# Two post-norm layers with a mixture of experts: norms and the last expert input on VectorE, the gates' parts behind the first gather, four more places for experts' weights

## The chip, the cores and the metric

The kernel runs as one program on one core of one Trainium2 chip. The metric is the device time of one execution in microseconds (us), the median of several runs. The engines are named as in the profile: PE (TensorE), PEld (its weight loads), DVE (VectorE), ACT (ScalarE), POOL (GpSimd) and SP (SyncE, which here only issues transfers).

## The reference

Two layers over 256 latent and 256 context tokens of width 1024. What follows the attention is what matters here:

```python
x = layer_norm(ALPHA * x + (1 + gate1) * o, ln1_g, ln1_b)       # ALPHA = 4 ** 0.25
u = x * (1 + scale2) + shift2                                   # input of the experts
if not last:                                                    # layer 0: context tokens too
    h_ctx = layer_norm(ALPHA * h_ctx + (1 + cgate1) * o_c, ln1_g, ln1_b)
    u_c = h_ctx * (1 + cscale2) + cshift2
f = moe_ffn(u, ...)        # 16 experts in 4 groups; best group, top 2 in it, gates normalised
x = layer_norm(ALPHA * x + (1 + gate2) * f, ln2_g, ln2_b)
```

In the experts, `hid = silu(xb @ w1[e]) * (xb @ w3[e])` and `y = (hid @ w2[e]) * gate`, in float32 with widths 1024, 512, 1024. Layer 0 sends 512 tokens through the experts, layer 1 only the 256 latent ones.

## The kernel before

A framework schedules the instructions by a model of their times; each engine and each transfer queue then works through its list in order, and waits at semaphores.

**Output projection and norm (`pre_moe`).** Tiles of 128 tokens, `n_out` of them (4 in layer 0, 2 in layer 1). For tile `t`, PE multiplies with `w_out` in two halves of 512 columns; its eight row blocks lie as split pairs: `wh`/`wl` (pool `wsp`, three pairs, blocks 0 to 2), `hl` in `ringb` (3 to 6) and `hl7` in pool `wos` (7). DVE builds the residual `z`. `post_norm` takes mean and variance of `z` (`stats`; ACT takes the square root), and writes three things: `u2` (the experts' input, with modulation; SP writes it to `u2d` in HBM, one transfer per tile), `xs` (the normed token, by ACT), and `xs` times ALPHA with the norm's gain and shift, which goes to `ysum` in HBM, where the experts' results are added. `lg` and `lb` hold the norm's gain and shift, multiplied by ALPHA on ACT beforehand. For all tiles but the last, the multiplication and addition of `xs` are done by POOL; for the last tile POOL makes `u2`, and DVE does `xs` later, after the first expert's indices (`keep["late"]` is ordered behind `keep["found"]`). `router` transposes `z` on PE, copies it on ACT (`zt`), and multiplies it with the router's weights into `lgt`; DVE turns that into `aff`.

**Routing (`route`).** A chain of small DVE instructions (`sel`, `hi`, `lo`, maxima, one-hots) gives the position of each token in its expert (`posm`) and the gates. The gates are cut into three bfloat16 parts by POOL (`auxg<-gate`), since PE sums them with one-hot matrices. For the first expert PE sums the tokens' numbers (`spare`), DVE turns them into indices (`ii`), and POOL gathers those rows of `u2d` with an indirect transfer (`xg<-u2d,ii`, the first gather). A one-element memset `mark` on POOL behind that gather releases transfers that are to come after it. Then all engines pass a branch (an overflow loop that isn't taken here).

**Experts (`moe`).** Weights come in units of 1024 KB, six per expert (two of each w1, w3, w2), 96 in a layer, loaded by SP (line 1303; 1289 for a unit in two halves) into places that take turns: 3 in `ring`, 4 in `ringu`, 4 in `ringb` (`n_slots` = 11), besides one unit in two halves in a `y` buffer and one in `xs`. The first 11 are issued before the gather: 10 as soon as their place is free, one (`PACE`) behind the last write of `u2d`. The unit in halves waits for `mark`, and all later units wait until a second `mark`, behind the second expert's gather, and the row of gates (`bcm`, or `xs<-modd` in layer 0) have been passed; each of these also waits until the unit four before it has landed (`DEPTH`). PE then multiplies: `ha`, `hb` (lines 1182, 1188) with w1 and w3, `ya`, `yb` with w2. PE's list has, ahead of the transposes of the first gather (`tp<-cst,xg`), the sums of the gates' parts (`ix<-auxg,oh`).

Of the kernel before, what the change touches and what calls it, by code (L numbers as in the profile page):

```python
# [17 lines left out]
F32 = mybir.dt.float32  # L18
# [5 lines left out]
ALU = mybir.AluOpType  # L24
# [4 lines left out]
P = 128  # L29
D = 1024  # L30
# [17 lines left out]
RING_B = 4  # L48
VECS_AHEAD = 2
# [3 lines left out]
PACE = (10, 11)  # L53
# [55 lines left out]
def layers(ctx: ExitStack, tc: tile.TileContext, x_in, x_ctx, c_in, w_in, w_out, w_ada, rows_in, lnv, sink, gains, rpbp,  # L109
# [344 lines left out]
    def pre_moe(l, sb, sr):  # L454
# [5 lines left out]
        with ExitStack() as st, ExitStack() as su:  # L460
# [429 lines left out]

            for tl in (lg, lb):
                S.mul(tl, tl, ALPHA)
# [35 lines left out]
            def post_norm(t, z):  # L928
# [3 lines left out]
                u2 = tmp.tile([P, D], F32, tag="u2", name="u2")  # L932
                if t < n_out - 1:
                    V.scalar_tensor_tensor(out=u2[:, half[0]], in0=z[:, half[0]], scalar=mean, in1=gg[:, half[0]],
                                           op0=ALU.subtract, op1=ALU.mult)
# [8 lines left out]
                else:  # L944

# [4 lines left out]
                    order(G.tensor_tensor(out=u2, in0=xs[:, t], in1=gg, op=ALU.mult), keep["normed"],  # L950
                          mybir.DependencyClass.NoSync)
                    G.tensor_tensor(out=u2, in0=u2, in1=bb, op=ALU.add)
                keep["u2 written"] = nc.sync.dma_start(u2d[t * P:(t + 1) * P], u2)
                eng = G if t < n_out - 1 else V
                keep["late"] = eng.tensor_tensor(out=xs[:, t], in0=xs[:, t], in1=lg, op=ALU.mult)
                keep["normed"] = eng.tensor_tensor(out=xs[:, t], in0=xs[:, t], in1=lb, op=ALU.add)
# [3 lines left out]
            def router(t, z, mean, y):  # L960
                r = t // 2
                for hf in range(2):
# [5 lines left out]
                    S.copy(zt, tp)  # L968
# [48 lines left out]
    def route(l, aff, nt, mp, ps):  # L1017
# [68 lines left out]
        V.tensor_tensor(out=gate, in0=chosen, in1=gsum.unsqueeze(2).to_broadcast(sh), op=ALU.mult)  # L1086
        for k in range(3):
            for r in range(nr):
                c = slice(2 * r, 2 * r + 2)
                part = aux[:, c, :, 2 + 3 * r + k]  # L1090
                G.tensor_copy(part, gate[:, c])
                if k < 2:
                    G.tensor_tensor(out=gate[:, c], in0=gate[:, c], in1=part, op=ALU.subtract)
# [160 lines left out]
    def moe(l, ringb, gen, rt, u2d, aff, nt, sb, ahead):  # L1254
        cap = CAP[l]
        with ExitStack() as st:
            mp = st.enter_context(tc.tile_pool(name="moe", bufs=1, side="right"))
            m1 = st.enter_context(tc.tile_pool(name="moe1", bufs=2))
# [18 lines left out]
            n_slots = RING_A + RING_U + RING_B  # L1277
# [6 lines left out]
            def eunit():  # L1284
                i = len(recent)
                src = order_of_use[loading[i]]
                if i == n_slots and Y_UNIT:
                    t = [gen.tile([P, D], F32, tag="y", name="w") for _ in range(2)]
                    d = [nc.sync.dma_start(t[k], src[:, k * 1024:k * 1024 + 1024]) for k in range(2)]
                    order(d[1], d[0], mybir.DependencyClass.NoSync)  # L1290
                    first_half.append(d[0])
                    d = d[1]
# [4 lines left out]

# [326 lines left out]
```

## Time and profile before

| | us |
|---|---|
| median of 3 runs (1178.72 to 1188.1) | 1181.44 |
| the profiled execution | 1177.92 |
| its span | 1176.1 |
| PE / DVE / ACT / POOL busy | 1047.7 / 524.5 / 333.5 / 291.4 |
| mean granted PE clock | 0.952 |

Layer 0 routes at 330 to 356 us and works through its experts until 637 us; layer 1 routes at 879 to 903 us, and its experts last until 1151 us. All times below are from the start of the span. In rows of a timeline the columns are start, duration, engine, line, operation, output and inputs, shape, count, and in brackets the idle time before and what ended it.

### The profile page before, as it was taken

How to read it: one execution, taken by the hardware profiler on the slowest of the kernel's cores; microseconds unless marked ns; L12 is line 12 of the kernel's file. 1: busy time of each engine (PE TensorE's matmuls, PEld its weight loads, DVE VectorE, ACT ScalarE, POOL GpSimd, SP SyncE). 2: the span in 40 equal slices, each digit the busy share in tenths (PEclk: the TensorE clock that was granted, in tenths of full speed). 3: DMA queues.
4: the chain of work that ended last, by engine and by line, in shares of the span. 5: the costliest groups of instructions: out<-in, count | busy, mean ns of one | idle time of the engine just before them, and what ended most of it. 6: DMA issues, size and time to landing. Idle time of an engine off the chain costs nothing. (4 is left out here: it accounts for less than half of the span.)

```text
span 1176.1 us, 21038 instructions
## 1 busy us (share of the span) xinstructions
PE 1047.7 (89%) x8651; PEld 606.3 (52%) x8652; DVE 524.5 (45%) x1207; ACT 333.5 (28%) x692; POOL 291.4 (25%) x250
## 2 busy tenths in 40 slices
PE   6999999999958999999996799999886998778875
PEld 4677666668844444444442578666663332223322
DVE  2435545655972444343333644655765221111114
ACT  1325457455221011011011543546531110000002
POOL 2000000100452434324313301001014453442242
PEclk9999999999968999999998799999985999998997
DMA  9854343856767999999996335656373999999992
GB/s 314 314 200 155 110 149 100 304 178 230 255 254 261 378 378 365 374 357 350 352 383 230 128 145 193 221 174 233 142 306 134 371 394 400 403 395 395 400 403 86
DMA packets 62161, 320.93 MB, mean 273 GB/s; under 512 B 14318, under 2 KB 18510, under 8 KB 28520
## 3 DMA queue, kind: packets, MB, share of 16 engines
q1 hardware_dynamic: 45120, 289.21, 64.6%
q0 software_dynamic: 11136, 23.30, 7.5%
q10 hardware_dynamic: 5800, 6.97, 1.8%
q8 instruction: 71, 1.16, 0.4%
q14 instruction: 34, 0.28, 0.1%
HBM read 310.40 MB, written 18.15 MB: 279 GB/s over the span
## 5 line engine op out<-in xcount | busy, mean ns | idle before, releaser
L1182 PE MATMUL ha<-w,xT 128*32 128x512 f32 (+1 forms) x1512 | 260.6, 615 | 31.1 <-DMA w<-in_w_dram 30.6
L1182 PEld LDWEIGHTS ha<-w,xT 128*32 128x32 f32 (+1 forms) x1512 | 77.0, 123 | 180.3 <-issue 120.7
L1209 ACT ACTIVATE hs<-ha 64x512 f32<-64x512 f32 x32 | 18.9, 591 | 417.5 <-PE ha L1182 417.5
L1182 PE MATMUL ya<-w,gT 128*32 128x512 f32 (+1 forms) x768 | 129.0, 597 | 4.0 <-DVE y L1229 1.6
L220 PE MATMUL pj<-wh,u 128*128 128x512 f32 (+2 forms) x256 | 95.5, 386 | 3.5 <-ACT wh L210 2.2
L221 PE MATMUL pj<-wl,u 128*128 128x512 f32 (+2 forms) x256 | 97.1, 380 | 0.7 <-DVE wl L211 0.7
L222 PE MATMUL pj<-wh,u 128*128 128x512 f32 (+2 forms) x256 | 94.1, 380 | 0.0
L1154 POOL MEMSET xg<- 96x1024 f32 (+1 forms) x32 | 30.2, 946 | 236.2 <-PE tp L1167 148.6
L1251 POOL DMA_INDIRECT ysum<-y,ii x30 | 44.4, 1479 | 154.8 <-DVE y L1232 105.7
L1229 DVE TENSOR_TENSOR y<-ya,gt 64x512 f32<-64x512 f32 x60 | 41.3, 688 | 84.9 <-PE ya L1182 77.3
L534 DVE TENSOR_REDUCE mx<-s 128x1 f32<-128x512 f32 (+1 forms) x80 | 54.8, 689 | 43.4 <-PE s L522 42.6
L1210 DVE TENSOR_TENSOR hs<-hs,ha 64x512 f32<-64x512 f32 x32 | 22.1, 690 | 114.3 <-ACT hs L1209 114.1
L545 ACT ACTIVATE p<-s,nm 128x512 f32<-128x512 f32 (+1 forms) x96 | 59.3, 623 | 37.4 <-DVE nm L541 21.5
L211 DVE TENSOR_TENSOR wl<-w,wh 128x1024 fp32r<-128x1024 f32 x38 | 46.0, 1222 | 48.7 <-ACT wh L210 48.7
L1182 PEld LDWEIGHTS ya<-w,gT 128*32 128x32 f32 (+1 forms) x768 | 35.1, 119 | 56.0 <-issue 46.9
L1188 PE MATMUL hb<-w,xT 128*32 128x256 f32 x1008 | 63.9, 379 | 0.0
L220 PEld LDWEIGHTS pj<-wh,u 128*128 128x128 f32 x256 | 48.6, 192 | 18.5 <-issue 4.3
L210 ACT CAST wh<-w 128x1024 fp32r<-128x1024 f32 x38 | 39.1, 1049 | 63.4 <-DMA w<-in_w_in_dram 40.3
L567 PE MATMUL o<-vt,pt 128*64 128x64 f32 x1280 | 52.5, 227 | 3.0 <-ACT pt L489 2.9
L221 PEld LDWEIGHTS pj<-wl,u 128*128 128x128 f32 x256 | 49.8, 194 | 10.4 <-DVE wl L211 1.9
L222 PEld LDWEIGHTS pj<-wh,u 128*128 128x128 f32 x256 | 49.3, 193 | 10.1 <-issue 1.1
L1237 POOL TENSOR_SCALAR gt<-xs,gs 96x1024 f32<-96x1024 f32 x16 | 53.5, 3341 | 0.0
(299 smaller groups left out, 1734.3 us busy)
## 6 DMA issues: line engine op xcount, KB each, us to landing
w<-in_w_dram SPq DMA_DIRECT2D x188, 1024.0 KB
w<-in_w_ada_dram SPq DMA_DIRECT2D x44, 1024.0 KB
w<-in_w_in_dram SPq DMA_DIRECT2D x16, 1024.0 KB
w<-in_w_out_dram SPq DMA_DIRECT2D x8, 1024.0 KB
early<-in_w_ada_dram SPq DMA_DIRECT2D x4, 1024.0 KB
y<-modd POOLq DMA_DIRECT2D x6, 512.0 KB, 4.7
u2d<-u SPq DMA_DIRECT2D x6, 512.0 KB
ysum<-xs ACTq DMA_DIRECT2D x6, 512.0 KB
```

Source lines behind the costliest of these rows:

```text
L211: keep["split"] = d = eng.tensor_tensor(out=lo, in0=w, in1=h.bitcast(F32), op=ALU.subtract)
L220: T.matmul(out_, ah, bh, start=start, stop=False)
L221: T.matmul(out_, ah, bl, start=False, stop=False)
L222: keep["product"] = T.matmul(out_, al, bh, start=False, stop=stop)
L534: greatest = V.reduce_max(out=mx[:, :nb], in_=s.rearrange("p (b k) -> p b k", b=nb), axis=AX.X)
L545: power = S.activation(out=p_[:, c * w:(c + 1) * w], in_=s[:, c * w:(c + 1) * w], func=AF.Exp, scale=scale, bias=bk.nm[:, c, i:i + 1], acc ...
L567: T.matmul(bk.o[q:q + 64, oc:oc + HD], pt[:, (c * nk + k) * P + q:(c * nk + k) * P + q + 64], vt[:, (2 * (nb - 1)) + k, v0:v0 + HD], start ...
L1182: keep["product"] = T.matmul(a[64 * m + t0:64 * m + t1], x[:, kt, t0:t1], w(m, kt), start=(kt == 0), stop=(kt == n - 1))
L1188: keep["product"] = T.matmul(b[c:c + self.cap - 64, 0:256], x[:, kt, 64:], w(m, kt)[:, hf * 256:hf * 256 + 256], start=(kt == 0), stop=(kt ...
L1229: V.tensor_tensor(out=out_[:n, half[m]], in0=a[64 * m:64 * m + n], in1=g[:n, half[m]], op=ALU.mult)
L1237: order(G.tensor_scalar(out=g[:self.cap], in0=self.bcs[0][:self.cap], scalar1=gs[:self.cap, 0:1], scalar2=None, op0=ALU.mult), keep["gathe ...
L1251: G.indirect_dma_start(dst, bass.IndirectOffsetOnAxis(ap=ii[:cap], axis=0), y[:cap], None, bounds_check=self.nt * P - 1, oob_is_err=False, ...
```

## The change

It does four things.

1. `lg` and `lb` are no longer multiplied by ALPHA; ALPHA is the scalar operand of a combined instruction (`scalar_tensor_tensor`). Both instructions on `xs` run on DVE for every tile, and `u2` of the last tile is made on DVE too. The pairs of tile 2 (layer 0) and of the last tile come after the first expert's indices. ACT's copy of the last tile's second half (`zt`) is ordered behind the square root.
2. The gates' parts on POOL are ordered behind the first gather.
3. There are 15 places instead of 11: three units lie in the `wh`/`wl` pairs (six loads of 512 KB), and one in a new pool `ringc`, which lies where `wos` lay.
4. Correspondingly 15 units are issued before the gather, and the unit that is held back behind the last write of `u2d` is number 14 instead of number 10.

```diff
+WS_UNITS = 3
-PACE = (10, 11)
+PACE = (14, 15)
...
-            for tl in (lg, lb):
-                S.mul(tl, tl, ALPHA)
...
+                V.scalar_tensor_tensor(out=u2[:, half[0]], in0=z[:, half[0]], scalar=mean, in1=gg[:, half[0]],
+                                       op0=ALU.subtract, op1=ALU.mult)
                 if t < n_out - 1:
...
                 else:
+                    V.scalar_tensor_tensor(out=u2[:, half[1]], in0=z[:, half[1]], scalar=mean, in1=gg[:, half[1]],
+                                           op0=ALU.subtract, op1=ALU.mult)
                     y, nmr = rstd()
...
-                    order(G.tensor_tensor(out=u2, in0=xs[:, t], in1=gg, op=ALU.mult), keep["normed"],
-                          mybir.DependencyClass.NoSync)
-                    G.tensor_tensor(out=u2, in0=u2, in1=bb, op=ALU.add)
+                    V.scalar_tensor_tensor(out=u2, in0=u2, scalar=y, in1=bb, op0=ALU.mult, op1=ALU.add)
                 keep["u2 written"] = nc.sync.dma_start(u2d[t * P:(t + 1) * P], u2)
-                eng = G if t < n_out - 1 else V
-                keep["late"] = eng.tensor_tensor(out=xs[:, t], in0=xs[:, t], in1=lg, op=ALU.mult)
-                keep["normed"] = eng.tensor_tensor(out=xs[:, t], in0=xs[:, t], in1=lb, op=ALU.add)
+                d = V.scalar_tensor_tensor(out=xs[:, t], in0=xs[:, t], scalar=ALPHA, in1=lg, op0=ALU.mult, op1=ALU.mult)
+                if t in (2, n_out - 1):
+                    keep.setdefault("late", []).append(d)
+                V.scalar_tensor_tensor(out=xs[:, t], in0=lb, scalar=ALPHA, in1=xs[:, t], op0=ALU.mult, op1=ALU.add)
...
-                    S.copy(zt, tp)
+                    d = S.copy(zt, tp)
+                    if hf and t == n_out - 1:
+                        order(d, keep["root"], mybir.DependencyClass.NoSync)
...
+            ringc = st.enter_context(tc.tile_pool(name="ringc", bufs=1))
...
-            n_slots = RING_A + RING_U + RING_B
+            slots = [(ring, "w")] * RING_A + [(ringu, "wu")] * (RING_U - 1) + [(ringb[0], "wb")] + [
+                (ringb[1], "wb")] * (RING_B - 1) + [None] * WS_UNITS + [(ringc, "wb"), (ringu, "wu")]
+            n_slots = len(slots)
...
+                slot = slots[i if i < n_slots else (i - XS_UNIT - Y_UNIT) % n_slots]
+                if i == n_slots and Y_UNIT or slot is None:
+                    t = [gen.tile([P, D], F32, tag="y", name="w") for _ in range(2)] if slot else [
+                        wsp.tile([P, 1024], F32, tag=tag, name="w") for tag in ("wh", "wl")]
...
-                order(keep["late"], keep["found"], mybir.DependencyClass.NoSync)
+                for d in keep["gate parts"]:
+                    order(d, first_gather, mybir.DependencyClass.NoSync)
+                for d in keep.pop("late"):
+                    order(d, keep["found"], mybir.DependencyClass.NoSync)
```

In layer 0, SP's list around the writes of `u2d` reads as follows before (units are `128x2048`, halves `128x1024`).

```order
L1303 DMA w<-in_w_dram 128x2048 x5
L953 DMA u2d_2951<-u_3060 128x1024
L953 DMA u2d_2951<-u_3168 128x1024
L1303 DMA w<-in_w_dram 128x2048 x4
L953 DMA u2d_2951<-u_3282 128x1024
L1303 DMA w<-in_w_dram 128x2048
L953 DMA u2d_2951<-u_3391 128x1024
L1303 DMA w<-in_w_dram 128x2048
```

The same place of SP's list in the change:

```order
L1308 DMA w<-in_w_dram 128x2048 x5
L950 DMA u2d_2951<-u_3058 128x1024
L1308 DMA w<-in_w_dram 128x2048
L950 DMA u2d_2951<-u_3166 128x1024
L1308 DMA w<-in_w_dram 128x2048 x4
L950 DMA u2d_2951<-u_3280 128x1024
L1299 DMA w<-in_w_dram 128x1024 x6
L1308 DMA w<-in_w_dram 128x2048
L950 DMA u2d_2951<-u_3389 128x1024
L1308 DMA w<-in_w_dram 128x2048
```

Ten units stand ahead of the third write in both, one of them now ahead of the second; between the third write and the last stand the three units in halves and the one in `ringc`. In layer 1 the same four units stand between the tenth unit and the first of that layer's two writes.

On POOL in layer 0, the list from tile 2 to the branch reads before:

```order
L955 TENSOR_TENSOR xs<-xs,xg 128x1024
L956 TENSOR_TENSOR xs<-xs,ln_2953 128x1024
L950 TENSOR_TENSOR u_3391<-xs,y 128x1024
L952 TENSOR_TENSOR u_3391<-u_3391,xg 128x1024
L1091 CAST auxg<-gate 128x32 x2
L1093 TENSOR_TENSOR gate<-gate,auxg 128x32 x2
L1091 CAST auxg<-gate 128x32
L1155 DMA xg<-u2d_2951,ii 96x1024
L1312 MEMSET mark 128x1
L1091 CAST auxg<-gate 128x32
L1093 TENSOR_TENSOR gate<-gate,auxg 128x32 x2
L1091 CAST auxg<-gate 128x32 x2
```

And in the change:

```order
L1157 DMA xg<-u2d_2951,ii 96x1024
L1317 MEMSET mark 128x1
L1093 CAST auxg<-gate 128x32 x2
L1095 TENSOR_TENSOR gate<-gate,auxg 128x32 x2
L1093 CAST auxg<-gate 128x32 x2
L1095 TENSOR_TENSOR gate<-gate,auxg 128x32 x2
L1093 CAST auxg<-gate 128x32 x2
```

The four large instructions are gone, and all ten for the gates' parts stand behind the gather and its mark; in layer 1 five stood ahead of the gather, and all five stand behind it now.

On ACT in layer 1, the end of the norm stands so before, and below so in the change (`sd` is the square root, `aff` the router's sigmoid).

```order
L968 COPY zt<-ztp 128x512 x2
L250 ACTIVATE sd<-mv,epsc 128x1
L947 ACT_TABLE_LOAD
L947 ACTIVATE sigmoid<-epsc 128x1
L949 ACTIVATE xs<-z,nmr,y 128x1024
```

```order
L967 COPY zt<-ztp 128x512
L956 DMA ysum_118<-xs 128x1024
L251 ACTIVATE sd<-mv,epsc 128x1
L946 ACT_TABLE_LOAD
L946 ACTIVATE sigmoid<-epsc 128x1
L967 COPY zt<-ztp 128x512
L948 ACTIVATE xs<-z,nmr,y 128x1024
```

The last `zt`, on which the last half of the logits waits, now stands behind the table load and the sigmoid.

More of the change, by code (lines that the diff above doesn't have):

```diff
@@ L932, in post_norm @@
                 u2 = tmp.tile([P, D], F32, tag="u2", name="u2")
+                V.scalar_tensor_tensor(out=u2[:, half[0]], in0=z[:, half[0]], scalar=mean, in1=gg[:, half[0]],
+                                       op0=ALU.subtract, op1=ALU.mult)
                 if t < n_out - 1:
-                    V.scalar_tensor_tensor(out=u2[:, half[0]], in0=z[:, half[0]], scalar=mean, in1=gg[:, half[0]],
-                                           op0=ALU.subtract, op1=ALU.mult)
                     y, nmr = rstd()
@@ L1086, in route @@
         V.tensor_tensor(out=gate, in0=chosen, in1=gsum.unsqueeze(2).to_broadcast(sh), op=ALU.mult)
+        keep["gate parts"] = parts = []
         for k in range(3):
@@ L1090, in route @@
                 part = aux[:, c, :, 2 + 3 * r + k]
-                G.tensor_copy(part, gate[:, c])
+                parts.append(G.tensor_copy(part, gate[:, c]))
                 if k < 2:
-                    G.tensor_tensor(out=gate[:, c], in0=gate[:, c], in1=part, op=ALU.subtract)
+                    parts.append(G.tensor_tensor(out=gate[:, c], in0=gate[:, c], in1=part, op=ALU.subtract))
         posm = tt("posm")
@@ L1286, in eunit @@
                 src = order_of_use[loading[i]]
-                if i == n_slots and Y_UNIT:
-                    t = [gen.tile([P, D], F32, tag="y", name="w") for _ in range(2)]
+                slot = slots[i if i < n_slots else (i - XS_UNIT - Y_UNIT) % n_slots]
+                if i == n_slots and Y_UNIT or slot is None:
+                    t = [gen.tile([P, D], F32, tag="y", name="w") for _ in range(2)] if slot else [
+                        wsp.tile([P, 1024], F32, tag=tag, name="w") for tag in ("wh", "wl")]
                     d = [nc.sync.dma_start(t[k], src[:, k * 1024:k * 1024 + 1024]) for k in range(2)]
                     order(d[1], d[0], mybir.DependencyClass.NoSync)
-                    first_half.append(d[0])
-                    d = d[1]
+                    if slot:
+                        first_half.append(d[0])
                 else:
@@ L1296, in eunit @@
                     else:
-                        j = i if i < n_slots else (i - XS_UNIT - Y_UNIT) % n_slots
-                        pool = (ring, "w") if j < RING_A else (ringb[j > RING_A + RING_U - 1], "wb") if (
-                            0 <= j - RING_A - RING_U + 1 < RING_B) else (
-                            ringu, "wu")
-                        t = pool[0].tile([P, 2048], F32, tag=pool[1], name="w")
-                    d = nc.sync.dma_start(t, src)
+                        t = slot[0].tile([P, 2048], F32, tag=slot[1], name="w")
+                    d = [nc.sync.dma_start(t, src)]
                     t = [t[:, k * 1024:k * 1024 + 1024] for k in range(2)]
-                recent.append(d)
                 if i >= n_first + AFTER:
-                    order(d, recent[i - DEPTH], mybir.DependencyClass.Sync)
+                    order(d[0], recent[i - DEPTH], mybir.DependencyClass.Sync)
+                recent.append(d[-1])
                 units[loading[i]] = t
```

## The prediction

> **What bounds the kernel now.** I read the busy table by stage first, then what PE waits for in each stage, then the timelines of DVE, POOL, ACT and SP around the two routings.
>
> ```profile
> 450.00:480.00 30.00, 29.79 (x362) 13.18 (x366) 12.40 (x28) 3.81 (x9) 11.51 (x8) 1.00 1.00 375
> 618.00:624.00 6.00, 4.59 (x30) 1.15 (x32) 1.28 (x1) 0.00 (x0) 3.69 (x2) 0.72 0.99 369
> 990.00:1020.00 30.00, 26.03 (x121) 9.37 (x123) 5.69 (x13) 2.48 (x6) 11.49 (x10) 1.00 1.02 404
> PE ha L1182 <- DMA w<-in_w_dram: 3.4, 2, 2.0
> PE ha L1182 <- DMA w<-in_w_dram: 10.3, 8, 2.8
> w<-in_w_dram SPq DMA_DIRECT2D x188, 1024.0 KB
> ```
>
> Columns of the first three: stretch, length, busy time of PE, PEld, DVE, ACT, POOL, granted PE clock, share of the DMA engines, GB/s. In layer 0's experts (450 to 480) PE is busy 29.79 of 30 us: PE is the bound. Only at the end (600 to 645, first wait row) does it wait for weights, 3.4 us, and the clock falls to 0.72. In layer 1's experts (990 to 1020) the transfer engines are full (1.02) at 404 GB/s and PE waits for weights, 10.3 us in 1000 to 1070 (second wait row): there the weights are the bound. A unit of 1024 KB is 1.049 MB and costs 2.60 us at 404 GB/s.
>
> So layer 0 pays for whatever delays its first expert, layer 1 for the moment at which the stream of weights starts for good and for how many units it still has to bring. Now the routing of layer 0:
>
> ```profile
> 331.21 0.16 DVE L257 RECIPROCAL y<-sd 128x1 f32<-128x1 f32 x1 [0.84 <-ACT sd L250]
> 333.62 0.17 DVE L977 TENSOR_TENSOR aff<-lgt,ms 128x16 f32<-128x16 f32 x1 [1.42 <-PE lgt L971]
> 333.90 2.39 POOL L950 TENSOR_TENSOR u<-xs,y 128x1024 f32<-128x1024 f32 x1 [5.38 <-ACT xs L949]
> 334.39 1.98 DVE L1024 TENSOR_TENSOR sel<-aff,rbb 128x64 f32<-128x64 f32 x1 [0.32 <-ACT aff L1012]
> 336.37 2.34 POOL L952 TENSOR_TENSOR u<-u,xg 128x1024 f32<-128x1024 f32 x1
> 336.40 2.35 DVE L1027 TENSOR_TENSOR hi<-sel 128x32 f32<-128x32 f32 x1
> 338.68 0.18 DVE L1028 TENSOR_TENSOR lo<-sel 128x32 f32<-128x32 f32 x1
> 338.73 0.33 SPq L953 DMA_DIRECT2D u2d<-u  x1
> 344.67 0.47 POOL L1091 CAST auxg<-gate 128x32 bf16<-128x32 f32 x2 [5.97 <-DVE most_i L1103]
> 345.15 0.15 DVE L1152 CAST ii<-fi 96x1 int32<-96x1 f32 x1
> 347.94 1.07 POOL L1155 DMA_INDIRECT xg<-u2d,ii  x1
> 350.38 0.41 PE L1138 MATMUL ix<-auxg,oh 128*96 128x6 bf16 x4 [0.75 <-POOL auxg L1091]
> 352.06 1.01 PE L201 MATMUL spare<-zeros 128*128 128x256 bf16 x4
> 356.06 1.51 PE L1167 MATMUL tp<-cst,xg 96*128 96x96 f32 x8 [2.99 <-DMA xg<-u2d,ii]
> ```
>
> `sel` and `hi` end when POOL's two large instructions end; `lo`, of the size of `hi`, takes 0.18. The indices are there at 345.3, the gather starts at 347.94, behind POOL's casts, and PE gets the rows 8.1 us later. POOL's parts last from 344.67 to 350.48 with the gather's 1.2 among them: 4.6. Layer 1:
>
> ```profile
> 882.35 0.59 ACT L968 COPY zt<-ztp 128x512 f32<-128x512 f32 x1 [2.00 <-PE ztp L966]
> 882.43 3.57 PE L971 MATMUL lgt<-wsc,zt 128*128 128x16 f32 x16 [0.17 <-DVE aff L977]
> 883.14 1.28 ACT L947 ACT_TABLE_LOAD   x1
> 886.03 0.17 DVE L977 TENSOR_TENSOR aff<-lgt,ms 128x16 f32<-128x16 f32 x1 [1.21 <-PE lgt L971]
> 886.24 2.31 DVE L978 SCALAR_TENSOR_TENSOR aff<-aff,y,wsum 128x16 f32<-128x16 f32 x1
> 888.84 2.14 DVE L1024 TENSOR_TENSOR sel<-aff,rbb 128x32 f32<-128x32 f32 x1 [0.29 <-ACT aff L1012]
> 896.12 0.15 DVE L1152 CAST ii<-fi 64x1 int32<-64x1 f32 x1
> 896.19 1.24 DVE L955 TENSOR_TENSOR xs<-xs,xg 128x1024 f32<-128x1024 f32 x1
> 896.42 1.15 POOL L1091 CAST auxg<-gate 128x32 bf16<-128x32 f32 x1
> 899.72 1.06 POOL L1155 DMA_INDIRECT xg<-u2d,ii  x1 [0.57 <-DVE gs L1143]
> 903.03 1.08 PE L1167 MATMUL tp<-cst,xg 64*128 64x64 f32 x8 [1.21 <-DMA xg<-u2d,ii]
> 907.37 1.83 POOL L1154 MEMSET xg<- 64x1024 f32 x2 [6.47 <-SPq L1352]
> 911.03 0.57 SPq L1303 DMA_DIRECT2D xs<-in_w_dram  x1
> ```
>
> From the gather to the first unit of the lasting stream (911.03) pass 11.3 us.
>
> **Layer 0, term by term.** *Indices.* Without POOL's pair, `sel` and `hi` cost about 0.2 each: 1.98 + 2.35 - 0.4 = 3.9 us gained. DVE's own new work on `u2` stands in waits that it has already: two instructions of half a row, some 0.65 each by half of the 1.24 below, where it waits 0.84 for the root, and one of 1.24 where it waits 1.42 for the logits. That leaves about 0.5. The last `zt` now waits for a table load, which costs some 1 us, but POOL's pair no longer delays the residual that feeds it; I set these three against each other, bounds 1 us either way. Indices at 341.4. If that cover is gone, these 2.5 us stand on the path.
>
> *The write of `u2d`.* DVE ends `u2` near 333, POOL did at 338.7. But SP's list puts four units, 4.19 MB, ahead of that write. Whether the write has to queue behind them no row shows; the transfer engines are full then, so I price it by order of issue.
>
> ```profile
> 308.00:312.00 4.00, 4.00 (x23) 3.37 (x22) 4.00 (x4) 0.59 (x1) 3.39 (x2) 1.00 0.35 134
> 328.00:332.00 4.00, 3.37 (x19) 3.08 (x18) 3.02 (x11) 2.17 (x4) 0.52 (x1) 0.65 1.02 426
> 332.00:336.00 4.00, 4.00 (x21) 3.25 (x21) 2.19 (x5) 2.07 (x4) 2.10 (x1) 0.50 0.70 288
> 880.00:884.00 4.00, 2.76 (x18) 2.48 (x17) 3.96 (x8) 1.98 (x4) 3.60 (x2) 0.77 0.38 153
> 884.00:888.00 4.00, 4.00 (x21) 3.38 (x21) 2.62 (x6) 1.87 (x3) 1.83 (x1) 0.50 0.00 0
> 900.00:904.00 4.00, 2.79 (x18) 1.72 (x16) 0.48 (x4) 1.70 (x3) 0.90 (x2) 0.50 0.74 227
> 904.00:908.00 4.00, 4.00 (x15) 1.41 (x15) 0.81 (x5) 0.15 (x1) 0.63 (x1) 0.50 0.41 156
> ```
>
> The queue runs full until about 334.5 (share 1.02, then 0.70). One unit moves into the gap at 308 to 312 (less 2.5 us), tile 2's write to `ysum` goes behind the indices (less 1.2), four units at 426 GB/s add 9.8: 340.6; the write itself 1.2; about 1 until its semaphore: 343. So the write, not the indices, now releases the gather, at 343 instead of 347.9. Bounds: 341.5, where the write does not queue and the indices decide, and 351.7, where the four units move at the 227 GB/s of the row at 900.
>
> *What is late next.* All ten gate parts now follow the gather, beside four DVE instructions of 1.2 us on `xs` instead of two. The cast at 896.42 shows how that goes: 1.15 us where it ends with DVE's. I keep their 4.6 us, between 2.8 (ten of 0.28, undisturbed as the pair at 344.67 nearly was) and 7; behind the gather's 1.2 they end near 348.8, and PE, whose list has the sums of these parts ahead of the transposes, comes to those 2.8 us later (350.3 to 353.07 before) at 351.6; the rows need 343 + 8.1 = 351.1. The first expert starts at 352 instead of 356.06: **4 us**, which PE-bound experts keep. The stalls at their end (3.4 us, and 6 us at clock 0.72, together about 5) have four more units in hand, worth some 10 us of lead; I take **4**. Layer 0: 8 us, bounds 2 and 11.
>
> **Layer 1.** *Indices.* `aff` and `sel` lose 2.31 + 2.14 - 0.4 = 4.0 us. Against it, tile 0's pair on `xs` (2 x 1.24, from the DVE row) now stands between residual and statistics, and the last `zt`, 882.35 before, comes behind the square root (near 883.5), the table load of 1.28 and the sigmoid, so at 885.3; it takes 0.59, and the last eight of the sixteen logit products at 882.43 take 1.8: 887.7 instead of 886.0. Net 4.0 - 1.7 = 2.3: indices at 894.0, bounds 892 and 896.
>
> *Write.* The queue empties at 881.6 (share 0.38 in 880 to 884) and lies idle till 888. Four units, `ysum` and the write: 881.6 + 9.8 + 1.2 + 1.2 + 0.7 = 894.5. Gather at 894.6, **5.1 us** earlier; I keep the 11.3 us behind it, since the parts (0.27 to 1.16 us each) fit into POOL's 6.47 us of waiting at the branch.
>
> *Stream.* Four units fewer: 4 x 2.60 = **10.4 us**. Fifteen of the later units come in halves. Per full share the halves at 904 to 908 moved 156 / 0.41 = 380 GB/s, against 404 / 1.02 = 396: 0.1 us per unit, 1.6 in all. PE starts only some 2.8 us before its 903.03 (its sums wait for the parts), while the stream wants places 5.1 us earlier; the first reloads wait for PE, and I charge 2. Layer 1: 5.1 + 10.4 - 1.6 - 2 = **12 us**, bounds 5 and 16. PE doesn't become the bound, since its waits for weights in 1000 to 1070 alone are 10.3.
>
> Moving ALPHA off ACT I cost at nothing: two instructions beside attention, with ACT 28% busy.
>
> **Two rules weighed.** For `sel`, the Trainium skill, SBUF — State Buffer, "SBUF: two separate sides", says that GpSimd and a VectorE instruction with two SBUF inputs hold a common port pair exclusively for a whole instruction. The trace agrees: 1.98 and 2.35 us, ended by POOL's. The rule also speaks against the change: with four late DVE instructions the first four parts would each wait 1.2 us, making the parts 2 us longer and layer 0 worth 6.
>
> Against the change speaks also the Trainium skill, DMA: Bandwidth & Descriptors, "Queues, rings and completion order": descriptors of one ring are consumed in order. By it the write of `u2d` stands behind all four units, as I priced; without it the gathers would leave at 341.5 and 894.1, 1.5 and 0.5 us sooner. No run here shows it.
>
> **Rivals.** (B) *The write eats the gather.* The indices come earlier but the gathers leave when they did, at 348 and 899.7. Then layer 0 keeps its 4 us of stalls, layer 1 10.4 - 1.6 = 9: 13 in all, 1167 on the scale of the last part. For it: 4 MB in a full queue. Against: both queues have idle stretches behind (0.00 at 884 to 888).
>
> (C) *Reloads wait for places.* The four units bring nothing in layer 1 because each reload needs the place that PE frees; the layer gains only PE's 2.8: 11 us, 1169. Against: PE waits for weights in every stretch there, so places are free.
>
> (D) *Slower: halves.* If fifteen units in halves move at 227 GB/s, as in 900 to 904, each costs 4.62 us, 2.0 more: 30 us in layer 1 and, past the 10 us of lead, 20 in layer 0: 1210. It is slower than now from 1.05 us more per unit on (15.8 + 5.8 against 20), below 287 GB/s. Against: the row's share is 0.74, so the engines idled for a quarter of it.
>
> **How the numbers follow.** 8 + 12 = 20 us off the profiled execution's 1177.92: 1158. The three timed runs were 1178.72 to 1188.1, their median 3.5 and their lowest 0.8 above the profiled execution; between the two I add 2 and predict 1160. Chances: forecast 0.55 (own range 1150 to 1167), B 0.22, C 0.16, D 0.07. The range goes down to both layers' upper bounds (11 + 16 = 27: 1151, less 3 for the spread of runs: 1148), and up past B and C to where layer 0 stays at its lower bound in them (6 more: 1175, and 2): 1177. D is out. A measurement here tells about 1% from no change: faster is below 1169.6 (the forecast, 0.15 of B, 0.07 of C: 0.77), within 1% 0.16, slower 0.07.
>
> **What would show it.** `sel` and `hi` under 0.4 us in both layers; the gather within 0.5 us of the indices or released by the write, at 343 and 894.6; PE's first transposes at 352 and 900, released by POOL's parts; no wait for weights in layer 0; in layer 1 no idle queue at 882 to 892, the stream for good from 906, and its last unit 12 us after less time. I am wrong if the write lands beyond 350 or 901, if the parts stretch past 352, or if the stream in layer 1 falls below 390 GB/s.

## The result: 1153.95 us, and the profile after

| | before | the change |
|---|---|---|
| median, first comparison (4 runs each) | 1184.77 us | 1153.95 us (1151.46 to 1155.49) |
| ratio, 95% interval | | 0.9735 [0.967, 0.980] |
| median, with the experiments (11 and 5 runs) | 1180.65 us | 1157.52 us (1154.79 to 1160.19) |
| ratio, 95% interval | | 0.9806 [0.9781, 0.9832] |
| span of the profiled execution | 1176.1 us | 1149.6 us |
| PE / DVE / ACT / POOL busy | 1047.7 / 524.5 / 333.5 / 291.4 | 1032.0 / 518.2 / 330.1 / 257.0 |

The change is 23 to 31 us faster; 1160 was predicted, in a range of 1148 to 1177. Where the 26.5 us between the two profiled spans lie is seen by cutting both at the same instructions. The cuts are starts of rows of the timelines: the first residual of a layer (`z<-oacc,y`, DVE), PE's first transposes of gathered rows (`tp<-cst,xg`), the last `hs` on ACT of a layer's experts, the first cast of layer 1's attention output (`o<-otp`, ACT), and the unit in `xs`, with which layer 1's lasting stream starts. The columns "again", "four places" and "eleven places" are kernels of the experiments.

| stretch, us | before | change | again | four places | eleven places |
|---|---|---|---|---|---|
| A: start to layer 0's first residual | 293.8 | 292.2 | 295.7 | 293.7 | 293.6 |
| B: to PE's first transposes | 62.2 | 59.8 | 59.9 | 60.6 | 60.8 |
| C: to layer 0's last `hs` | 279.1 | 271.2 | 271.4 | 274.6 | 280.3 |
| D: to layer 1's first cast of the attention output | 208.4 | 210.0 | 211.7 | 211.3 | 212.1 |
| E: to layer 1's first residual | 25.3 | 18.9 | 20.5 | 25.2 | 19.8 |
| F: to layer 1's lasting stream | 42.2 | 41.1 | 39.9 | 41.7 | 39.4 |
| G: to layer 1's last `hs` | 239.1 | 230.5 | 230.4 | 229.6 | 239.6 |
| H: to the end | 26.0 | 25.9 | 25.8 | 25.8 | 26.7 |

A and D hold attention, in which nothing was predicted to move; between "change" and "again", which are the same kernel, they differ by 3.5 and 1.7 us, with a mean granted clock of 0.962 and 0.950 over the whole execution. So only B, C, E, F and G are read below. Against the predicted 4, 4, 0, 5.1 and 6.8 they gave 2.4, 7.9, 6.4, 1.1 and 8.6.

The routing of layer 0 in the change, from the timelines of DVE, POOL, PE and SP:

```profile
332.88 0.23 DVE L1025 TENSOR_TENSOR sel<-aff,rbb 128x64 f32<-128x64 f32 x1 [0.32 <-ACT aff L1013]
333.14 0.19 DVE L1028 TENSOR_TENSOR hi<-sel 128x32 f32<-128x32 f32 x1
333.88 0.33 SPq L950 DMA_DIRECT2D u2d<-u  x1
339.73 0.15 DVE L1154 CAST ii<-fi 96x1 int32<-96x1 f32 x1
339.80 2.35 DVE L952 SCALAR_TENSOR_TENSOR xs<-xs,xg 128x1024 f32<-128x1024 f32 x2
342.06 2.35 DVE L955 SCALAR_TENSOR_TENSOR xs<-ln,xs 128x1024 f32<-128x1024 f32 x2
345.21 0.56 DVE L1131 TENSOR_TENSOR oh<-cst,posm 128x384 bf16<-128x384 f32 x1 [0.79 <-DMA u2d<-u]
346.07 1.05 POOL L1157 DMA_INDIRECT xg<-u2d,ii  x1 [34.36 <-DVE oh L1131]
347.17 0.77 POOL L1093 CAST auxg<-gate 128x32 bf16<-128x32 f32 x2
349.14 0.47 POOL L1093 CAST auxg<-gate 128x32 bf16<-128x32 f32 x2
347.21 0.21 PE L1138 MATMUL ix<-cbf 128*96 128x6 bf16 x1 [7.71 <-PEq L1360]
349.52 0.41 PE L1140 MATMUL ix<-auxg,oh 128*96 128x6 bf16 x4 [2.10 <-POOL auxg L1093]
352.01 1.49 PE L1169 MATMUL tp<-cst,xg 96*128 96x96 f32 x8
```

`sel` and `hi` are down to 0.23 and 0.19 us, and the indices come at 339.73 instead of 345.15. But the gather leaves only at 346.07, 0.9 us after DVE's wait for the last write of `u2d` has ended (345.21). Before, it left 2.8 us behind the indices, now 6.3; against the layer's first residual it leaves when it did (53.9 us behind it, 54.1 before). What B gains lies behind the gather: PE's transposes follow it after 5.9 us, 8.1 before. The gates' parts take 2.4 us. PE comes past the branch at 347.21 (7.71 us behind its last work, 4.49 before), waits 2.10 for the parts, and no longer for the rows.

The same in layer 1, with PE's wait for the parts there, and then the windows (busy time by engine, granted clock, share of the transfer engines, GB/s):

```profile
878.20 0.14 DVE L1154 CAST ii<-fi 64x1 int32<-64x1 f32 x1
881.50 0.49 DVE L1131 TENSOR_TENSOR oh<-cst,posm 128x128 bf16<-128x128 f32 x2 [0.76 <-DMA u2d<-u]
882.21 1.03 POOL L1157 DMA_INDIRECT xg<-u2d,ii  x1 [44.60 <-DVE oh L1131]
893.22 0.58 SPq L1308 DMA_DIRECT2D xs<-in_w_dram  x1
```

```profile
884.96 0.22 PE L1140 MATMUL ix<-auxg,oh 128*64 128x3 bf16 x2 [3.90 <-POOL auxg L1093]
```

```profile
336.00:340.00 4.00, 0.99 (x18) 0.81 (x17) 3.54 (x28) 0.00 (x0) 0.00 (x0) 0.73 1.04 420
344.00:348.00 4.00, 0.21 (x1) 0.23 (x2) 1.53 (x3) 0.97 (x1) 1.92 (x5) 0.50 1.03 395
612.00:618.00 6.00, 6.00 (x82) 2.72 (x76) 2.07 (x3) 0.00 (x0) 2.81 (x1) 1.00 0.67 236
876.00:880.00 4.00, 1.05 (x10) 0.56 (x8) 3.68 (x18) 0.00 (x0) 0.00 (x0) 0.86 1.02 423
888.00:892.00 4.00, 4.00 (x17) 1.57 (x18) 0.81 (x5) 0.37 (x1) 2.29 (x3) 0.50 0.04 17
930.00:1100.00 170.00, 144.28 (x700) 53.39 (x697) 31.77 (x76) 14.02 (x35) 69.04 (x45) 0.98 1.02 395
```

The same view of before:

```profile
336.00:340.00 4.00, 1.03 (x10) 0.88 (x9) 3.83 (x14) 0.00 (x0) 2.62 (x2) 0.93 0.12 48
612.00:618.00 6.00, 3.99 (x44) 1.35 (x36) 3.06 (x6) 0.48 (x1) 0.68 (x1) 1.00 1.01 397
950.00:1120.00 170.00, 140.98 (x646) 51.29 (x644) 30.02 (x70) 13.11 (x32) 64.01 (x42) 0.97 1.02 399
```

The transfer engines are full until 348 in layer 0, where they idled at 336 to 340 before (share 0.12), and until some 883 in layer 1; then they stand idle at 888 to 892. From 612 to 618 PE is busy all the time, where it was busy for 3.99 of 6 us before. In layer 1's experts the engines run at 395 GB/s with 15 units in halves (399 before).

What the prediction didn't look at is stretch E. The timelines of ACT and PE at the end of layer 1's attention, before and then in the change:

```profile
850.37 0.59 ACT L867 CAST o<-otp 128x512 fp32r<-128x512 f32 x1 [5.21 <-PE otp L864]
854.89 1.06 ACT L892 ACTIVATE ln<-ln 128x1024 f32<-128x1024 f32 x1 [3.93 <-DMA ln<-in_lnv_dram]
855.85 0.57 ACT L867 CAST o<-otp 128x512 fp32r<-128x512 f32 x1
856.32 4.83 ACT L913 CAST hl<-w 128x1024 fp32r<-128x1024 f32 x5
857.41 2.08 PE L220 MATMUL oacc<-hl,o 128*128 128x512 f32 x4 [6.64 <-ACT hl L913]
```

```profile
840.02 1.07 ACT L868 CAST o<-otp 128x512 fp32r<-128x512 f32 x2 [5.21 <-PE otp L865]
840.98 4.85 ACT L911 CAST hl<-w 128x1024 fp32r<-128x1024 f32 x5
842.09 1.19 PE L221 MATMUL oacc<-hl,o 128*128 128x512 f32 x4 [1.67 <-ACT hl L911]
```

Before, the multiplication of `ln` by ALPHA stood between two casts in ACT's list, and its row of HBM landed 3.93 us after ACT came to it. The last cast and the five casts of `w_out`'s blocks, for which PE waits, stood behind it: 5.4 us passed from the end of the `o` cast at 850.37 to the first `hl` cast, and in the change the `hl` casts follow the `o` casts without a wait. PE's wait for them falls from 6.64 to 1.67 us.

### The profile page after: what moved, and what is told of

The parts are those of the page before. It is cut to its first block, busy times and chain, and to the rows that moved or that the text cites. A ratio compares the mean times of both kernels' runs of the same rounds, so it can differ in the third digit from the quotient of the medians.

```text
span 1149.6 us, 21044 instructions
## 1 busy us (share of the span) xinstructions
PE 1032.0 (90%) x8651; PEld 598.5 (52%) x8652; DVE 518.2 (45%) x1221; ACT 330.1 (29%) x688; POOL 257.0 (22%) x238
## 5 line engine op out<-in xcount | busy, mean ns | idle before, releaser
L1184 PE MATMUL ha<-w,xT 128*32 128x512 f32 (+1 forms) x1512 | 251.1, 604 | 22.1 <-DMA w<-in_w_dram 21.7
L1184 PEld LDWEIGHTS ha<-w,xT 128*32 128x32 f32 (+1 forms) x1512 | 74.4, 121 | 165.3 <-issue 117.0
L1211 ACT ACTIVATE hs<-ha 64x512 f32<-64x512 f32 x32 | 18.9, 592 | 403.4 <-PE ha L1184 403.4
```

The lines of the kernel that those rows point to most:

```text
L1184: keep["product"] = T.matmul(a[64 * m + t0:64 * m + t1], x[:, kt, t0:t1], w(m, kt), start=(kt == 0), stop=(kt == n - 1))
```

## The experiments

Twelve kernels. Medians stand beside the kernel before on the same chip, whose median was 1180.65, 1181.43, 1180.50 and 1184.02 us in the four groups.

**The change again** (the base of the others).

> The change itself once more, as the base for the three kernels beside it, which start from it. Both theories: 1154 us, ratio to the kernel before 0.9735, and the events of layer 0's and layer 1's routing within 0.5 us of the first profile of the change.

Measured: 1157.52, ratio 0.9806 [0.9781, 0.9832]; stretches B, C and G within 0.2 us of the first profile, E and F 1.6 longer and 1.2 shorter. Layer 1's indices and gather came 1.0 and 1.6 us sooner against the first residual, so not all events lay within the 0.5 us expected. Differences of 3 us between medians are therefore read from the stretches.

**ALPHA on ACT again.**

```diff
+            for tl in (lg, lb):
+                S.mul(tl, tl, ALPHA)
-                ... scalar=ALPHA, in1=lg ...
+                ... scalar=1.0, in1=lg ...
```

> The change with one part undone: the norm's gain and shift are again multiplied by ALPHA on ACT (two instructions a layer, where they stood before), and the combined instructions on DVE get the scalar 1.0. Theory of the profiles: in layer 1 ACT waits some 4 us for the shift's transfer ahead of that multiplication, the last cast of the attention's output stands behind it in ACT's list, and PE's projection waits for the cast; the two profiles lie 10.3 us apart ahead of that place and 16.7 behind it, so the time rises by 5 us (3 to 6.4), to 1159, the wait shows again as ACT ln <- DMA ln of 3 to 5 us, and the time from the end of layer 1's attention to its first residual is 6 us longer. Rival, the prediction's own term: the multiplication costs nothing, 1154 within 1 us, and the 4 to 6 us come from the norms' move.

Measured: 1166.64, ratio 0.988 [0.9857, 0.9904]: 9.1 us slower than the change beside it. The timeline of ACT:

```profile
227.64 1.06 ACT L893 ACTIVATE xg<-xg 128x1024 f32<-128x1024 f32 x1 [7.32 <-DMA xg<-in_lnv_dram]
854.91 1.06 ACT L893 ACTIVATE ln<-ln 128x1024 f32<-128x1024 f32 x1 [3.90 <-DMA ln<-in_lnv_dram]
```

Stretch E is 25.1 us again. And there is a second such wait, in layer 0's attention: 7.32 us for the gain (2.57 before, at 222.95), behind which PE's work fell back by some 5 us at 228. So the prediction's "nothing" was 4.6 us in E (20.5 to 25.1), which is shown. The median rose by 9.1 us where 5 were expected; that layer 0 has the rest rests on this one profile, since A lies anywhere between 292.2 and 298.1 in kernels without the multiplication.

**The kernel before, with the multiplication later.**

```diff
-            for tl in (lg, lb):
-                S.mul(tl, tl, ALPHA)
+            muls = [S.mul(tl, tl, ALPHA) for tl in (lg, lb)]     # ordered behind the last cast of w_out
```

> The kernel before with one thing moved: ACT multiplies the norm's gain and shift by ALPHA behind its last cast of the projection's weights instead of ahead of the last cast of the attention's output; all else as before. Theory: ACT's waits of 2.6 us (layer 0, attention) and 3.9 us (layer 1) for those two rows vanish; layer 1's first residual comes 5 to 6 us sooner after the attention, layer 0's attention up to 2.5 us; 6 us faster than before, ratio 0.995 (0.993 to 0.997). Rival, the prediction's term: nothing, ratio 1.000 within 0.002.

Measured: 1177.93, ratio 0.9968 [0.9943, 0.9993]. Stretch E fell from 25.3 to 19.0 us, as expected; but layer 0's stretch from the residual to the indices grew from 51.3 to 55.6, so that 3.5 us are left in the median where 6 were expected. One row of DVE holds most of that growth:

```profile
325.44 5.23 DVE L944 SCALAR_TENSOR_TENSOR u<-u,y,xg 128x512 f32<-128x512 f32 x2 [1.83 <-DMA xg<-modd]
```

Before, the same two instructions on tile 2's `u2` took 1.41 us, with no wait. Now they wait for a row that POOL asked for 4.4 us later (at 318.33 instead of 313.93), and run beside POOL's instructions on `xs` (324.98 to 330.12). Why POOL came later stays open. Layer 1's 6 us are shown from this side too; that the whole change gains them in the total isn't shown by this kernel, but by the one that undoes it.

**The write of `u2d` ahead of units 10 to 14.**

```diff
-PACE = (14, 15)
+PACE = (10, 15)        # and the first half of a unit in halves is held too
```

> The change with another order in SP's list: the five last units ahead of the gather (10 to 14) all stand behind the last write of u2d, where only unit 14 stood before. Theory of the ring's order: the write waits behind the units issued ahead of it, so now it lands some 9 us earlier, and the indices release the gather: layer 0 at 340.5 instead of 346.1, layer 1 about 3.5 us earlier against the indices' time. In layer 0 PE passes the branch at 347 anyway, so its first transposes come only 2 us earlier (350); in layer 1 the stream starts 3 us earlier: 1149 in all, between 1147 and 1152. Rival one: the transfer engines share their time among all that is issued, the write lands when the queue runs dry whatever the order, and the gather stays at 346 within 1 us: 1154. Rival two: the units that come later are missed by PE at the first expert, and what the gather gains is lost again there: 1154 to 1157, with waits for weights at 355 to 380 us.

Measured: 1157.61, ratio 0.9821 [0.9796, 0.9846]: nothing gained. POOL, DVE and PE in layer 0:

```profile
341.12 5.17 POOL L1157 DMA_INDIRECT xg<-u2d,ii  x1 [28.23 <-DVE ii L1154]
340.75 2.34 DVE L952 SCALAR_TENSOR_TENSOR xs<-xs,xg 128x1024 f32<-128x1024 f32 x2
343.02 2.35 DVE L955 SCALAR_TENSOR_TENSOR xs<-ln,xs 128x1024 f32<-128x1024 f32 x2
354.45 1.51 PE L1169 MATMUL tp<-cst,xg 96*128 96x96 f32 x8 [3.00 <-DMA xg<-u2d,ii]
```

The gather leaves 0.4 us behind the indices instead of 6.2, so the write did wait for the units ahead of it in its ring. This is what the Trainium skill, DMA: Bandwidth & Descriptors, "Queues, rings and completion order", says of one ring, and what no run had shown before. But POOL's gather lasts 5.17 us instead of 1.05, just past the end of DVE's four instructions, and the rows land later than in the change (B: 61.0). In layer 1 the gather leaves 0.9 us behind the indices, but F is 42.9: the stream starts 17.7 us behind the gather instead of 11.0, and POOL waits 9.20 us for SP's pass of the branch (4.63 in the change). Why SP passes so late is open. None of the three theories named DVE.

**All parts ahead of the gather.**

```diff
-                    order(d, first_gather, mybir.DependencyClass.NoSync)
+                    order(first_gather, d, mybir.DependencyClass.NoSync)
```

> The change with one part undone more than before: all of the gates' parts stand ahead of the first gather on POOL, instead of all of them behind it. Theory of the profiles: the write of u2d, not POOL, releases the gather at 346.1, 6 us after the indices, and the parts fit into those 6 us even beside DVE's four late instructions; so the gather stays within 0.5 us, PE's sums find their parts done, and PE's transposes come up to 1.5 us earlier in layer 0: 1152.5, between 1151 and 1154.5. Rival, by the prediction's reckoning of the parts (2.8 to 7 us on the path): the gather leaves 3 us later in layer 0 and 1.5 us later in layer 1: 1158.

Measured: 1160.26, ratio 0.9835 [0.9808, 0.9862]; B 59.9, F 40.5: the same as the change in both layers. The gather leaves 7.3 us behind the indices instead of 6.2, and PE's transposes follow it 1.0 us sooner. Neither the gain of the theory nor the rival's gather 3 us later came. The second part of the change is worth nothing that shows, in either direction.

**Eleven places.**

```diff
-WS_UNITS = 3
+WS_UNITS = 0           # no ringc, PACE = (10, 11)
```

> The change with its third and fourth part undone: eleven places and the old hold on unit 10; norms, ALPHA and the gates' parts as in the change. Theory of the profiles: the four places are worth layer 0's end (the first hidden instruction of its last expert comes 7.4 us earlier against the first expert in the change than before) and 8.4 us in layer 1's stream; but without the four units ahead of the write, the indices release the gather, 6 us earlier in layer 0 and 3.5 us in layer 1, of which PE keeps about 4 and 2. Sum 16 less 6: 10 us slower than the change, 1167 (1163 to 1172). Rival, the prediction's terms: places worth 4 + 10.4 - 1.6 - 2 = 10.8, gathers earlier by only 1.5 and 0.5: 9 us slower, 1166, but with less than 2 us between the gathers of the two kernels. The gathers tell the two apart: 6 us or under 2 us after the indices in the change.

Measured: 1173.56, ratio 0.9916 [0.9881, 0.9951], 16 us above the change's median (on another chip) where 10 were expected. C and G are 9 us longer each (280.3 and 239.6), so the places are worth 18 us. The gathers did leave with the indices (0.4 and 0.9 us behind), but that gave nothing in layer 0: B is 60.8, and the gather's row is long again.

```profile
341.88 5.16 POOL L1157 DMA_INDIRECT xg<-u2d,ii  x1 [28.77 <-DVE ii L1154]
354.40 1.51 PE L1169 MATMUL tp<-cst,xg 96*128 96x96 f32 x8 [2.30 <-DMA xg<-u2d,ii]
```

The transfer engines were idle then (share 0.02 at 340 to 344), so a full queue isn't what makes it long.

**`u2` of the last tile on POOL.**

```diff
-                    V.scalar_tensor_tensor(out=u2, in0=u2, scalar=y, in1=bb, op0=ALU.mult, op1=ALU.add)
+                    G.tensor_tensor(out=u2, in0=xs[:, t], in1=gg, op=ALU.mult)
+                    G.tensor_tensor(out=u2, in0=u2, in1=bb, op=ALU.add)
```

> The change with one part undone: the last tile's u2 is made by two POOL instructions again; everything else is as in the change. Theory of the profiles: aff, sel and hi last 2 us each again and the indices come 4 us later in layer 0 and 2.5 to 4 us in layer 1, but the gather waits for the full queue anyway (6 us and 4 us behind the indices in the change), so it stays within 1 us in both layers: 0 to 1.5 us slower, 1157 to 1159 beside 1157.5. Rival, the prediction's terms: 3.9 us in layer 0 and 2.3 us in layer 1 come back, 6 us slower: 1163.5.

Measured: 1165.49, ratio 0.9837 [0.979, 0.9883], 8 us above the change's median: the theory is refuted, though its first half holds. The indices came 3.3 us later in layer 0 and 3.4 or more in layer 1 (51.0 and 29.5 us behind the first residual, 47.5 to 47.7 and 25.1 to 26.1 in the change), and the gathers left about when they did (53.8 and 30.1; in the two profiles of the change 53.9 and 54.0, 30.1 and 28.4). But what follows came later (B 64.9, F 44.0). In layer 0 the four late DVE instructions start behind the indices: the gather leaves when the first two have ended (350.35), which the profile names as what it waited for, and runs beside the last two. The transfer engines were full until some 350 too, so its late start isn't shown to be DVE's. In layer 1 the stream starts 13.9 us behind the gather instead of 11.0, with DVE's late pair beside a gather of 1.60 us; the two kernels with eleven places, which differ in DVE's order alone, have 13.6 and 11.1.

```profile
350.73 2.83 POOL L1156 DMA_INDIRECT xg<-u2d,ii  x1 [9.52 <-DVE xs L951]
```

**Units held behind the gather's mark** (12 to 14 in layer 0, 13 and 14 in layer 1).

```diff
+                for d in heads[n_slots - HELD[l]:n_slots]:
+                    order(d, mark, mybir.DependencyClass.Sync)
```

> A version that may beat the change: the last units ahead of the gather (12 to 14 in layer 0, 13 and 14 in layer 1) are issued only behind the gather's mark, behind the unit in two halves; everything else is as in the change. Theory: what holds the gather's rows is the transfer queue, which runs full until 347.5 us in layer 0 and 882 us in layer 1, whatever stands first in it; with 7.9 MB less ahead of it in all, the queue runs dry near 340 and 877, the gather leaves within 1 us of the indices and its rows land 5 to 6 us later. PE starts 4 us earlier in layer 0; in layer 1 the stream for good starts 3 us earlier, and the held units fill the idle stretch of the queue that follows the branch: 6 us faster than the change, 1151 (1149 to 1154). Rival one: layer 0 lacks the held units at its end, waits for weights come back there (4 us), and only layer 1 gains: 1154 to 1155. Rival two: the queue's idle time merely moves ahead of the gather, and nothing changes: 1157.

Measured: 1170.75, ratio 0.9894 [0.9846, 0.9943]: 13 us slower than the change. The gathers left 1.2 and 1.3 us behind the indices, but B is 60.9, with a gather of 4.38 us beside DVE's late instructions. C is 278.9, with 2.5 us of waits for weights: layer 0 lacks the held units. F is 44.7: in layer 1, where SP issues them ahead of its branch, the stream starts 18.4 us behind the gather instead of 11.0. Rival one was right on layer 0; that layer 1 would gain was not.

**The gather ahead of DVE's late instructions, eleven places.**

```diff
-                    order(d, keep["found"], mybir.DependencyClass.NoSync)
+                    order(d, mark, mybir.DependencyClass.Sync)
```

> The kernel with eleven places, and DVE's late instructions on xs behind the gather's mark in both layers; so the transfer queue is empty when the gather leaves, and only DVE's part differs. Theory: DVE's four instructions hold the gather's descriptors; the gather's row in layer 0 goes from 5.16 us to 1.1, and PE's first transposes come 3 to 4 us earlier, 57 us after the first residual instead of 60.8 (they then wait for the gates' parts, which run beside DVE's instructions until some 7 us behind the indices); 3 to 4 us faster than the kernel with eleven places, 1170 beside 1173.5. Rival: something else makes the gather slow there (code that POOL has to fetch, the write's landing): the row stays near 5 us and nothing is gained.

Measured: 1164.24, ratio 0.9851 [0.9813, 0.9889], 9 us faster than with eleven places (on another chip), where 3 to 4 were expected; B 58.0 instead of 60.8, F 36.3 instead of 39.4, so 6 of the 9 are seen in these two stretches.

```profile
343.07 1.04 POOL L1157 DMA_INDIRECT xg<-u2d,ii  x1 [28.21 <-DVE ii L1154]
353.40 1.49 PE L1169 MATMUL tp<-cst,xg 96*128 96x96 f32 x8
```

Only DVE's order differs, and the gather's row goes from 5.16 to 1.04 us, while PE no longer waits for rows. That DVE's late instructions hold the gather is shown. A second pair says the same: in layer 0 the kernel with the write first and the next one below differ in DVE's order alone, and the gather takes 5.17 and 1.04 us, B 61.0 and 58.3. That it is their two inputs in SBUF no run shows, since none varies them. The Trainium skill, SBUF — State Buffer, "SBUF: two separate sides", describes this trap for a transfer issued by GpSimd, whose descriptors GpSimd writes, and for VectorE in a two-port mode; here instructions in float32 with two inputs did it.

**The same with fifteen places, the write first in layer 0.**

> A version that may beat the change. In layer 0 units 10 to 14 stand behind the last write of u2d (as in the kernel with the write first), and DVE's four late instructions on xs come behind the gather's mark instead of right behind the indices; layer 1 is as in the change. Theory: in the kernel with the write first, the gather's instruction on POOL lasted 5.17 us, as long as DVE's four late instructions beside it, instead of 1.05, and its rows moved only after that; so here it lasts 1.1 us again, its rows land 8 us after the indices as in that kernel's layer 1, and PE's first transposes come 3 us earlier against layer 0's first residual than in the change (56.5 to 57.5 us after it, not 59.7): 3 us faster, 1154.5 beside 1157.5. Rival: the full queue alone holds the rows; the gather's row on POOL gets short, but PE's transposes stay 59 to 61 us behind the residual: 1157 to 1158.

Its edit joins those of the write-first kernel (layer 0) and of the last one (layer 0). Measured: 1159.03, ratio 0.9811 [0.9777, 0.9845]: the same as the change. B is 58.3, 1.5 us shorter, with a gather of 1.04 us; but C is 276.0. A row of SP's timeline, and one of PE's waits in 470 to 625 us (total, times, longest):

```profile
362.99 0.37 SPq L1308 DMA_DIRECT2D xs<-in_w_dram  x1
PE ha L1184 <- DMA w<-in_w_dram: 2.3, 2, 1.4
```

PE starts earlier, but the lasting stream of layer 0 doesn't: 69.3 us behind the first residual, 67.4 in the change (359.61). What PE gains it loses again at the end of the layer: the last `hs` comes 334.3 us behind the first residual (B and C together), 331.0 in the change.

**Four places alone, on the kernel before.**

```diff
+WS_UNITS = 3           # slots, ringc and eunit() as in the change
-PACE = (10, 11)
+PACE = (14, 15)
```

> The kernel before with the third and fourth part alone: fifteen places, and the hold on unit 14; norms, ALPHA on ACT and the gates' parts as before. Theory of the profiles: the places are worth 8.9 us from layer 0's first expert to its last and 9.2 us from the start of layer 1's lasting stream to its last expert, as between the change and the kernel with eleven places; of this the fuller queue takes back 0 to 3 us at the gathers: 16 to 18 us, ratio 0.986 (0.984 to 0.988). Rival, the prediction's terms: 4 in layer 0 and 10.4 - 1.6 - 2 = 6.8 in layer 1, 11 us, ratio 0.991.

Measured: 1163.80, ratio 0.9843 [0.9806, 0.988]: 16.7 us, in total as the theory said. G is worth 9.5 us, near the 9.2 expected, but C only 4.5 of 8.9, and B 1.7. C keeps 3.4 us over the change's 271.2 and a wait for weights of 2.1 us: layer 0's lasting stream starts 69.6 us behind the first residual (363.35), not 67.4. This suggests that the change's other parts pay in layer 0 at its stream (2.2 us sooner) and not only at PE's first expert (B 0.8).

**Two units behind the branch.**

> A version that may beat the change, in layer 1 alone: of the fifteen units ahead of the gather, the last two are issued only behind the branch, ahead of the row of gates, and DVE's late pair comes behind the gather's mark; layer 0 is as in the change. Theory: the write of u2d then lands with the indices, as in the kernel with eleven places, so the gather leaves 3 us earlier; the stream for good starts 36.5 to 38 us behind layer 1's first residual instead of 40 to 41, and the two units (5.2 us) fill the 6 us that the transfer engines stand idle between the branch and that stream: 3 to 4 us faster, 1153.5 to 1154.5 beside 1157.5. Rival: the two units stand ahead of the second gather's rows and of the row of gates in the engines, and the stream starts no earlier than in the change, so that the two units are simply late: 1157.5 to 1160.

Measured: 1164.00, ratio 0.982 [0.9773, 0.9867]. The kernel doesn't do what was meant: in SP's list the two units stand ahead of the write in layer 1, not behind the branch. So it shows the opposite case: with all but half a unit ahead of the write, the gather leaves 5.1 us behind the indices (4.0 and 3.4 in the change) and F is 45.4. Whether the idle time at 888 to 892 can be filled stays open.

## Why the prediction was right, and where not

The direction, the bound (layer 1 by weights, layer 0 by PE) and the largest term held. One term that is worth some 6 us was put at nothing, and the others were mis-sized by up to 4 us each, in both directions.

*Indices.* Right in layer 0: 3.8 us earlier against the first residual (51.3 to 47.5), 3.9 predicted. In layer 1 it was 1.2 and 2.2 in the two profiles, 2.3 predicted. But the gathers didn't follow them.

*The write.* The mechanism was right, the size not. Predicted: the write of `u2d` releases the gather 1.6 us behind the indices in layer 0 and 0.6 in layer 1. Measured: 6.3 and 4.0 (6.2 and 3.4 in the second profile).

In layer 0 the step that failed is the gap that was to be filled ("less 2.5 us"). In the 10 us from its start (14 to 24 us behind the first residual) the transfer engines moved no more than before: 191 GB/s (196 in the second profile), where it was 221. One unit was issued there (311.85), but the four behind it came 24.9 us behind the first residual, 20.2 before. That is 2.5 of the 4.7 us by which the gather came late (53.9 us behind the first residual, 49.2 by the prediction). The sum's 1 and 0.7 us until the write's semaphore are in no row by themselves; the gather left 0.9 and 0.7 us after DVE's wait for the same write had ended.

In layer 1 the price of the units ahead of the write was too small. The gather left 30.1 and 28.4 us behind the first residual, and 25.8 was predicted. The queue ran full until 30 to 31 us behind it. Less unit 14, which stands behind the write (2.6), and the write itself (1.2), that leaves 26 to 27, where 24 had been added up. The norm's earlier start isn't the reason: with ALPHA on ACT again, where E is 25.1 us as before, the gather still left 3.3 us behind the indices and 28.8 behind the first residual. What took the 2 to 3 us is open.

So rival B's mechanism, the write that eats the gather, did happen: wholly in layer 0 (54.1 us before, 53.9 now), largely in layer 1 (30.9 before). F gained 1.1 us (2.3 in the second profile) where 5.1 was predicted. The total came out far below B's 1167 all the same, since layer 0's end and ALPHA gave more than B had for them.

*The parts.* Predicted 4.6 us beside four DVE instructions, measured 2.4: the late write kept them apart, DVE had ended at 344.4. That PE's transposes come at 352.01, as predicted, is chance: attention was 1.6 us faster in that profile, and B gained 2.4, not 4, by rows that were there sooner behind a gather as late as before. Why they were, no run shows. In layer 1 PE waits 3.90 us for the parts, and its first transposes come 35.4 us behind the first residual (33.9 in the second profile), 34.2 before, where 31 was predicted. Behind the gather or ahead of it, the parts cost the same.

*Layer 0's end.* 4 predicted, 7.9 measured; no wait for weights is left, as said. The stalls in the last expert were read rightly, as about 5 us: from `hs` to `hs` it took 29.1 us before and 24.0 now.

```profile
606.08 0.59 ACT L1209 ACTIVATE hs<-ha 64x512 f32<-64x512 f32 x1 [13.78 <-PE ha L1182]
635.16 0.59 ACT L1209 ACTIVATE hs<-ha 64x512 f32<-64x512 f32 x1 [19.42 <-PE ha L1182]
```

```profile
599.21 0.59 ACT L1211 ACTIVATE hs<-ha 64x512 f32<-64x512 f32 x1 [13.78 <-PE ha L1184]
623.22 0.59 ACT L1211 ACTIVATE hs<-ha 64x512 f32<-64x512 f32 x1 [14.35 <-PE ha L1184]
```

The step that failed is that the stalls were sought there alone ("only at the end"), and that 4 of the 5 were taken: 2.2 us more lay in the experts before, most of them in one that took 19.0 us (569.82 to 588.79) where the change takes 17.3, and 0.6 ahead of the first `hs`. Four places alone give 4.5 of the 7.9.

*Layer 1's stream.* 10.4 less 1.6 for halves was 8.8; G fell by 8.6. The 2 us for reloads waiting for places were not paid, so rival C is out, and the stream ran at 395 GB/s: D is out. The last unit was issued 26.4 us earlier (end of SP's row at 1141.66 and 1115.22), not 12; 16.7 of that lie ahead of layer 1's first residual, so that the layer itself gained 9.7.

```profile
1062.11 79.55 SPq L1303 DMA_DIRECT2D w<-in_w_dram  x30
```

```profile
1101.06 14.16 SPq L1308 DMA_DIRECT2D w<-in_w_dram  x6
```

*ALPHA.* The term that was wrong outright: "two instructions beside attention, with ACT 28% busy" at nothing. It is 6.4 us in E (4.8 in the second profile), and 9 us in the median of the experiment that undoes it. A busy share says nothing on an instruction that waits: before, `ln<-ln` waited 3.93 us for a transfer, in a list where PE's operands stood next.

Sum of the read stretches: 2.4 + 7.9 + 6.4 + 1.1 + 8.6 = 26.4, where 20 was predicted. Without ALPHA it is 20.0, and that is luck: B and F gave 5.6 us less than predicted, C and G 5.7 us more.

## What to carry to other kernels

Before an instruction is priced at nothing because its engine has time, look up what it waits for and what stands behind it in that engine's list. A transfer brought forward past a full queue gains only what the next thing in the chain allows: here the write, then DVE's late instructions, then the restart of the stream each took its turn. Cut two profiles at the same instructions and compare the stretches; a total that comes out right can hide terms that are wrong by as much as the effect.

## What the runs showed of the hardware that was not expected

- Layer 0's first gather took 1.04 to 1.07 us on POOL alone, and 5.16, 5.17, 4.38 and 2.83 us where DVE's float32 instructions with two inputs in SBUF ran beside it. With eleven places the transfer engines stood idle meanwhile (share 0.02 at 340 to 344). PE's first transposes came 2.8 us sooner once DVE's were moved behind the gather.
- With the write of `u2d` ahead of the last five units in SP's list the gather left 0.4 us behind the indices; with four of them ahead of the write it left 6.2 us behind.
- The same row of HBM, loaded in layer 0's attention, came 2.57 us after ACT asked for it in one kernel and 7.32 in another.
- Two executions of one kernel differ in attention alone: stretch A took 292.2 and 295.7 us, at a granted clock of 1.00 and 0.99 there (0.962 and 0.950 over the whole execution).
